# The split weights' second half computed by GpSimd in the mixers, and the vector products' weight tiles loaded by the sync engine

## The chip, the cores and the metric

The kernel runs on one core of a Trainium2 chip. The metric is device time in microseconds (us) for one execution. The kernel before took 3869.05 us (median of three runs, 3862.45 to 3869.21). A core has five engines that each run their own instructions in order: TensorE (PE, matrix products), VectorE (DVE), ScalarE (ACT), GpSimd (POOL) and SyncE (SP, here only a sequencer that issues DMAs). They wait for one another by semaphores. A DMA is an instruction of the engine that issues it, so it stands in that engine's row of work until what it waits for has come.

## The reference

Two blocks in a row, on x of 512 tokens by 1024 features and, in the first block, a context of 256 tokens, all in fp32. Cut to what matters here:

```
for l in 0, 1:                                           # first block
    m_lat = split(silu(c)     @ w_mod[l] + b_mod[l], 6)  # 6 x 1024 numbers: matrix times VECTOR
    m_ctx = split(silu(c_ctx) @ w_mod[l] + b_mod[l], 6)
    h  = rmsnorm(x)  * (1 + m_lat[1]) + m_lat[0]
    hc = rmsnorm(cx) * (1 + m_ctx[1]) + m_ctx[0]
    p, pc = h @ w_in[l], hc @ w_in[l]                    # 30 blocks of 128 columns
    mix = concat(neighbourhood_attention(p), gated_linear_scan(p), gated_conv(p))
    x = x + m_lat[2] * (mix @ w_out[l])
    x = x + m_lat[5] * mixture_of_experts(rmsnorm(x) * (1 + m_lat[4]) + m_lat[3])
    # layer 0: the same for the context
# second block: FFN, differential attention, FFN, shared keys and values,
# FFN, forgetting attention, FFN; each with shifts, scales and gates out of
# silu(c) @ ada_w[layer] (9 x 1024 numbers), one more out of silu(c) @ kv_ada_w
```

## The kernel before, in words

Activations lie transposed, 128 features by the tokens. Each weight projection is done to nearly full fp32 accuracy with three fast products: a weight tile `raw` is rounded by ScalarE into `wh` (L244), its rest `wl = raw - wh` is taken by VectorE (L245), the activation is split the same way, and `mm3` (L247 on) adds `wh*hh + wh*hl + wl*hh` for each 128-row slab (L252, L253, L254). One `split` of 8 slabs makes two pairs of `wh` and `wl`, each 128x512.

A mixer (`mixers`, `mix_in`) is the stage of layer l from `h` to `mix`. `mix_in` runs over 15 loads of 1 MB from `w_in` (`raw`, L117, issued by SyncE, two buffers), two column blocks each. So a mixer has 30 splits, that is 60 roundings and 60 subtractions of 128x512. The `wp` pool holds three pairs (`bufs=3`) of four slabs. Between column blocks run the scan (`hgrn`, lines 676 to 850), the neighbourhood attention (L543 to L601) and the convolution, with much work on VectorE.

The matrix-vector products (`gemv`, L155 to L182) are background work. Each step loads a tile `g` of 128x1024 (512 KB, L166, two buffers), and VectorE multiplies it by the broadcast condition `cb` and sums along the row (L174, output `junk`; 512 wide in the first block, two halves and up to two targets, latent and context, a tile). `fill` inserts steps of these jobs at a set rate between column blocks or FFN tiles: products with `w_mod` in the two mixers and just behind them, with `ada_w` from mixer 1 to FFN 1 (1024 wide there), with `kv_ada_w` near the shared keys and values. `paced` orders each of these instructions behind the last `mm3` matmul issued so far; only the first two loads of a job wait for that matmul on the chip.

The order on each engine comes from the framework's scheduler: the program order with priorities. `later` pushes the splits of `mix_in` back (or the column work as a whole), so that attention and scan go first where both are ready. Once set, each engine runs in that order.

Stages in the profiled execution: mixer 0 to about 500 us, mixture of experts 0 to about 980, mixer 1 to about 1400, mixture of experts 1 to about 1780, then FFN 0 (to 2140), differential attention, FFN 1 (2440 to 2790), keys and values, FFN 2, forgetting attention, FFN 3.

Of the kernel before, what the change touches and what calls it, by code (L numbers as in the profile page):

```python
# [9 lines left out]
F32 = mybir.dt.float32  # L10
# [4 lines left out]
OP = mybir.AluOpType  # L15
# [46 lines left out]
class Net:  # L62
# [95 lines left out]
    def gemv(self, wT, tiles, targets):  # L158


        nc = self.nc
        before = None
        for t in list(tiles) + [None]:
            if t is not None:
                g = self.gp.tile([128, D], F32, tag="g", name="g")
                self.paced(nc.gpsimd.dma_start(g, wT[t]), t - tiles[0] < 2)  # L166
            if before is not None:
                for cb, dst, bias in targets:
                    at = dst[:, before[1]:before[1] + 1]
                    w = self.junk.shape[-1]  # L170
                    part = self.sp.tile([128, 2], F32, tag="part", name="part", bufs=4)
                    for j in range(D // w):
                        js = slice(w * j, w * j + w)
                        self.paced(nc.vector.scalar_tensor_tensor(self.junk, before[0][:, js], 1.0, cb[:, js], op0=OP.mult,  # L174
                                                                  op1=OP.mult, accum_out=part[:, j:j + 1] if w < D else at))
                    if w < D:
                        nc.vector.tensor_add(at, part[:, 0:1], part[:, 1:2])
            if t is None:
                for cb, dst, bias in targets:
                    lo, hi = tiles[0], tiles[-1] + 1  # L180
                    nc.vector.tensor_add(dst[:, lo:hi], dst[:, lo:hi], bias[:, lo:hi])
            before = g, t  # L182
            yield
# [45 lines left out]
                                 self.vec("b_mod0", 0, 16).rearrange("p (j k) -> p j k", k=4))  # L229


    def split(self, src, nk):

        hi, lo = [], []
        for k0 in range(0, nk, 4):
            n = min(4, nk - k0)
            wh, wl = (self.wsplit.tile([128, 4, 128], F32R, tag=n, name=n) for n in ("wh", "wl"))
            self.split_act(src[:, k0:k0 + n], wh[:, :n], wl[:, :n])
            hi += [wh[:, k] for k in range(n)]
            lo += [wl[:, k] for k in range(n)]  # L240
        return hi, lo

    def split_act(self, src, hi, lo):
        self.nc.scalar.activation(hi, src, AF.Copy)  # L244
        self.nc.vector.tensor_tensor(lo, src, hi.bitcast(F32), op=OP.subtract)  # L245

    def mm3(self, out, w, h, ks, first=True, last=True):  # L247
        nc = self.nc
# [181 lines left out]
    def mix_in(self, l, h, hc, na, hg, cv, mix, mixc, need):  # L430
        nc = self.nc
        w = self.a[f"w_in{l}"]
        for f2 in range(15):
            raw = self.raw(w[f2]).rearrange("p (e k m) -> p e k m", e=2, k=8)
            for e in range(2):
                n, p = ORDER[2 * f2 + e]
                ctx = need or n in ("nk", "nv", "hf", "hb", "hi")
                with self.later(-LATER - 400 if l + f2 + e == 0 else -1000):
                    ws = self.split(raw[:, e], 8)
                b, bc = self.bank("m"), self.bank("m")[:, :TC] if ctx else None  # L440
                for ks in (range(4), range(4, 8)):
                    for o, v in ((b, h), (bc, hc)):
                        if o is not None:
                            self.mm3(o, ws, v, ks, ks[0] == 0, ks[-1] == 7)
                if n[0] == "n":
                    for key, s in (("l", b), ("c", bc)):
                        if s is not None:
                            t = na[p][n, key] = self.tmp("ev" if key == "l" else "evc", s.shape[-1])
                            nc.scalar.activation(t, s, AF.Copy)
                elif n[0] == "c":  # L450
                    self.conv(l, n, p, b, bc, cv[p], mix, mixc)
                else:
                    if n in ("hf", "hb"):
                        if n == "hf":
                            hg[p]["z"] = self.tmp("hz", 4 * TA).rearrange("p (s t) -> p s t", s=4)
                        t = hg[p]["z"][:, 0 if n == "hf" else 3]
                    else:
                        t = hg[p][n] = self.tmp(n, TA)
                    for s, sl in ((bc, slice(0, TC)), (b, slice(TC, TA))):
                        if s is None:  # L460
                            continue
                        if n == "hg":
                            nc.scalar.activation(t[:, sl], s, AF.Silu)
                        else:
                            nc.scalar.activation(t[:, sl], s, AF.Copy, scale=0.125 if n == "hq" else 1.0)
                self.fill(self.rate)
                yield
# [1239 lines left out]
```

## Time and profile before

| what | value |
|---|---|
| runs | 3869.05, 3869.21, 3862.45 us |
| profiled execution | 3865.91 us, span 3864.0 us, granted clock 0.965 |
| PE busy | 3628.6 us (94%), 21140 matmuls |
| VectorE busy | 2182.7 us (56%), 5476 instructions |
| ScalarE busy | 1444.8 us (37%) |
| GpSimd busy | 156.0 us (4%), 273 instructions |
| all `wl` on VectorE (L245) | 558.8 us, 826 of them |
| all `wh` on ScalarE (L244) | 512.0 us, 826 of them |
| `g` loads on GpSimd (L166) | 240 of 512 KB |

Busy shares are means over stages that differ: VectorE has 56% in the whole span, but far more in the mixers, and less in the FFNs. PE's records overlap, since matmuls are pipelined, so that its busy share tells little of how much room it has; the number of matmuls in a window tells more. "Idle before" is time in which an engine had nothing to run, with what ended it. A DMA instruction counts as busy only for its issue (about half a us on GpSimd, a third on SyncE); the transfer comes after.

### The profile page before, as it was taken

The page shows a single profiled execution, that of the slowest core. Times are in us where ns is not written, and L with a number is a line of the kernel's source. Part 1 is how long each engine was busy: PE and PEld are TensorE (multiplying, and loading weights), DVE is VectorE, ACT ScalarE, POOL GpSimd, SP SyncE. Part 2 cuts the span into 40 slices and gives each one's busy share as a digit, 9 for nine tenths or more (in the row PEclk, how much of TensorE's full clock was granted, in tenths as well). Part 3 has the DMA queues.
Part 4 walks back from the last instruction along what each step waited for, and adds up shares of the span by engine and source line. Part 5 has one row for each costly group of instructions (what it writes and reads, how often), then busy time and mean ns, then how long its engine had stood idle before and what let it go on. Part 6 is the DMA issues. An engine that isn't in the chain of part 4 may idle for free. (4 is left out here: it accounts for less than half of the span.)

```text
span 3864.0 us, 54771 instructions
## 1 busy us (share of the span) xinstructions
PE 3628.6 (94%) x21140; PEld 2640.8 (68%) x21140; DVE 2182.7 (56%) x5476; ACT 1444.8 (37%) x2826; POOL 156.0 (4%) x273
## 2 busy tenths in 40 slices
PE   7999998999899998988999998999989999999998
PEld 4777784333577775436888676788778887677887
DVE  4999874222689864215566665655643334664334
ACT  4566431111466641113233454322343223553222
POOL 0000000000000000000010000001100000000000
PEclk8999998999899998999999998999999999999999
DMA  5222265777433476994555221455522222012222
GB/s 204 73 80 93 93 209 184 297 278 264 155 118 115 157 238 241 359 344 147 196 196 185 89 77 58 154 191 206 186 76 88 98 103 86 34 55 87 95 96 82
DMA packets 154197, 588.03 MB, mean 152 GB/s; under 512 B 18048, under 2 KB 57256, under 8 KB 111952
## 3 DMA queue, kind: packets, MB, share of 16 engines
q1 hardware_dynamic: 113760, 442.43, 32.0%
q0 software_dynamic: 37872, 137.90, 10.4%
q10 hardware_dynamic: 2304, 4.20, 0.3%
q8 instruction: 166, 2.72, 0.3%
q14 instruction: 95, 0.78, 0.1%
HBM read 575.01 MB, written 9.46 MB: 151 GB/s over the span
## 5 line engine op out<-in xcount | busy, mean ns | idle before, releaser
L244 ACT ACTIVATE wh<-raw 128x512 fp32r<-128x512 f32 (+1 forms) x826 | 512.0, 622 | 1231.9 <-PE m L253 859.0
L245 DVE TENSOR_TENSOR wl<-raw,wh 128x512 fp32r<-128x512 f32 (+1 forms) x826 | 558.8, 678 | 711.0 <-ACT wh L244 698.3
L252 PE MATMUL m<-h,wh 128*128 128x512 f32 x1632 | 658.9, 404 | 26.5 <-DVE t L323 8.4
L253 PE MATMUL m<-h,wh 128*128 128x512 f32 x1632 | 657.7, 403 | 6.2 <-DVE h L326 5.4
L254 PE MATMUL m<-h,wl 128*128 128x512 f32 x1632 | 658.9, 404 | 1.1 <-DVE wl L245 1.1
L174 DVE SCALAR_TENSOR_TENSOR junk<-g,cb 128x512 bf16<-128x512 f32 (+1 forms) x440 | 374.6, 851 | 26.3 <-DMA g<-in_modT 18.5
L252 PEld LDWEIGHTS m<-h,wh 128*128 128x128 f32 x1632 | 313.9, 192 | 99.6 <-ACT h L325 19.0
L253 PEld LDWEIGHTS m<-h,wh 128*128 128x128 f32 x1632 | 312.8, 192 | 81.6 <-DVE h L326 16.5
L254 PEld LDWEIGHTS m<-h,wl 128*128 128x128 f32 x1632 | 312.9, 192 | 68.9 <-issue 7.0
L254 PE MATMUL m<-e,wl 128*128 128x512 f32 x832 | 325.5, 391 | 7.9 <-DVE wl L245 7.9
L252 PE MATMUL m<-e,wh 128*128 128x512 f32 x832 | 325.2, 391 | 0.5 <-ACT wh L244 0.5
L253 PE MATMUL m<-e,wh 128*128 128x512 f32 x832 | 324.7, 390 | 0.0
L252 PE MATMUL f<-h,wh 128*128 128x512 f32 x768 | 299.5, 390 | 0.0
L254 PE MATMUL f<-h,wl 128*128 128x512 f32 x768 | 299.1, 389 | 0.0
L253 PE MATMUL f<-h,wh 128*128 128x512 f32 x768 | 299.0, 389 | 0.0
L1111 PE MATMUL m<-raw,xg 128*64 128x512 f32 (+1 forms) x1264 | 255.0, 603 | 11.0 <-DMA raw<-in_exp_gu 11.0
L254 PEld LDWEIGHTS m<-e,wl 128*128 128x128 f32 x832 | 156.9, 189 | 40.8 <-DVE wl L245 8.3
L1111 PEld LDWEIGHTS m<-raw,xg 128*64 128x64 f32 (+1 forms) x1264 | 63.7, 125 | 173.2 <-issue 146.5
L252 PEld LDWEIGHTS m<-e,wh 128*128 128x128 f32 x832 | 157.1, 189 | 33.4 <-ACT wh L244 1.2
L253 PEld LDWEIGHTS m<-e,wh 128*128 128x128 f32 x832 | 156.9, 189 | 32.7
L254 PEld LDWEIGHTS f<-h,wl 128*128 128x128 f32 x768 | 144.4, 188 | 30.3 <-DVE wl L245 0.3
L252 PEld LDWEIGHTS f<-h,wh 128*128 128x128 f32 x768 | 144.4, 188 | 30.0 <-issue 0.2
(456 smaller groups left out, 5149.9 us busy)
## 6 DMA issues: line engine op xcount, KB each, us to landing
raw<-in_exp_gu SPq DMA_DIRECT2D x98, 1024.0 KB, 6.8
raw<-in_ffn_in SPq DMA_DIRECT2D x88, 1024.0 KB, 4.7
g<-in_adaT POOLq DMA_DIRECT2D x144, 512.0 KB, 4.0
raw<-in_exp_dn SPq DMA_DIRECT2D x48, 1024.0 KB, 6.8
g<-in_modT POOLq DMA_DIRECT2D x80, 512.0 KB, 3.7
raw<-in_w_in SPq DMA_DIRECT2D x30, 1024.0 KB, 4.8
raw<-in_ffn_out SPq DMA_DIRECT2D x32, 896.0 KB, 4.5
raw<-in_ffn_out SPq DMA_DIRECT2D x16, 1024.0 KB, 4.7
```

Of the source, the lines that this page charges most:

```text
L174: self.paced(nc.vector.scalar_tensor_tensor(self.junk, before[0][:, js], 1.0, cb[:, js], op0=OP.mult, op1=OP.mult, accum_out=part[:, j:j + ...
L244: self.nc.scalar.activation(hi, src, AF.Copy)
L245: self.nc.vector.tensor_tensor(lo, src, hi.bitcast(F32), op=OP.subtract)
L252: nc.tensor.matmul(out, wh[k], hh[k], start=(first and k == ks[0]), stop=False)
L253: nc.tensor.matmul(out, wh[k], hl[k], start=False, stop=False)
L254: self.last = nc.tensor.matmul(out, wl[k], hh[k], start=False, stop=(last and k == ks[-1]))
L1111: self.nc.tensor.matmul(out[es, c:c + n], xg[:, es], t, start=start, stop=stop)
```

## The change

Three places. `split` gets an argument `rest`, the engine that takes the subtraction; only `mix_in` gives one, GpSimd. So the 120 subtractions of both mixers move from VectorE to GpSimd; those of the FFNs, attentions and output projections stay. The `g` loads of `gemv` are issued by SyncE in place of GpSimd, all 240 of them, in every stage. The broadcast loads of `cb`, six memsets of `kv` and the indirect row loads of the experts stay on GpSimd.

```diff
@@ gemv
-                self.paced(nc.gpsimd.dma_start(g, wT[t]), t - tiles[0] < 2)
+                self.paced(nc.sync.dma_start(g, wT[t]), t - tiles[0] < 2)
@@ split, split_act
-    def split(self, src, nk):
+    def split(self, src, nk, rest=None):
...
-            self.split_act(src[:, k0:k0 + n], wh[:, :n], wl[:, :n])
+            self.split_act(src[:, k0:k0 + n], wh[:, :n], wl[:, :n], rest)
...
-    def split_act(self, src, hi, lo):
+    def split_act(self, src, hi, lo, rest=None):
         self.nc.scalar.activation(hi, src, AF.Copy)
-        self.nc.vector.tensor_tensor(lo, src, hi.bitcast(F32), op=OP.subtract)
+        (rest or self.nc.vector).tensor_tensor(lo, src, hi.bitcast(F32), op=OP.subtract)
@@ mix_in
-                    ws = self.split(raw[:, e], 8)
+                    ws = self.split(raw[:, e], 8, self.nc.gpsimd)
```

On GpSimd, at the start of mixer 0, the row of instructions changes as follows (L733 clears `kv`, L151 loads the broadcast condition):

```order
+L245 TENSOR_TENSOR wl<-raw,wh 128x512 x3
 L733 MEMSET kv 128x1536
+L245 TENSOR_TENSOR wl<-raw,wh 128x512
 L151 DMA cb<-in_c 128x1024
+L245 TENSOR_TENSOR wl<-raw,wh 128x512 x2
 L151 DMA cb<-in_c_ctx 128x1024
-L166 DMA g<-in_modT 128x1024 x6
+L245 TENSOR_TENSOR wl<-raw,wh 128x512 x13
 L733 MEMSET kv 128x1536
-L166 DMA g<-in_modT 128x1024 x11
```

The subtractions take the places that the `g` loads had, between the same memsets and broadcast loads; GpSimd's row has 38 lines in place of 37.

On SyncE, in the first part of mixer 0 (`nb` are the tables of the attention's bias):

```order
-L117 DMA raw<-in_w_in 128x2048 x5
+L117 DMA raw<-in_w_in 128x2048
+L166 DMA g<-in_modT 128x1024
+L117 DMA raw<-in_w_in 128x2048
+L166 DMA g<-in_modT 128x1024 x2
+L117 DMA raw<-in_w_in 128x2048
+L166 DMA g<-in_modT 128x1024 x3
+L117 DMA raw<-in_w_in 128x2048
+L166 DMA g<-in_modT 128x1024 x3
+L117 DMA raw<-in_w_in 128x2048
+L166 DMA g<-in_modT 128x1024 x4
```

Where the weight loads stood in a row, one to four `g` loads now stand between two of them, and a load behind a `g` load that waits is issued after it. In the FFNs two `g` loads stand between two weight loads.

On VectorE, in mixer 0 around the first gates of the scan (L682 to L701):

```order
-L245 TENSOR_TENSOR wl<-raw,wh 128x512
 L682 SCALAR_TENSOR_TENSOR ls<-hz,ls 128x1536
 L174 SCALAR_TENSOR_TENSOR junk,part<-g,cb 128x512
 L683 TENSOR_TENSOR hz<-ls,hz 128x2x768
 L697 SCALAR_TENSOR_TENSOR hz<-ones,ls 128x128 x12
-L245 TENSOR_TENSOR wl<-raw,wh 128x512
+L174 SCALAR_TENSOR_TENSOR junk,part<-g,cb 128x512
 L700 COPY hsmall<-hz 128x12
-L245 TENSOR_TENSOR wl<-raw,wh 128x512
+L177 TENSOR_TENSOR mlat_82<-part 128x1
+L174 SCALAR_TENSOR_TENSOR junk,part<-g,cb 128x512
```

The subtractions go, and the products with `g` move forward into their places; scan and attention keep their order among themselves.

## Rows read from the trace of the kernel before

**Rows 1.** the page, part 1: busy us, share of the span, instructions.

```profile
PE 3628.6 (94%) x21140; PEld 2640.8 (68%) x21140; DVE 2182.7 (56%) x5476; ACT 1444.8 (37%) x2826; POOL 156.0 (4%) x273
```

**Rows 2.** windows, mixers and FFN 1: length, busy PE PEld DVE ACT POOL, clock, DMA, GB/s.

```profile
87.00:498.00 411.00, 393.03 (x4229) 309.47 (x4229) 382.64 (x1221) 227.05 (x508) 22.82 (x40) 0.99 0.27 92
1050.00:1390.00 340.00, 319.66 (x3093) 245.21 (x3091) 304.55 (x941) 213.68 (x431) 29.80 (x53) 0.97 0.42 142
2450.00:2750.00 300.00, 300.00 (x1325) 248.51 (x1324) 177.24 (x282) 92.82 (x153) 29.56 (x56) 1.00 0.55 194
```

**Rows 3.** lines by form, VectorE, mixer 0: busy us, mean ns, idle before.

```profile
L174 DVE SCALAR_TENSOR_TENSOR junk<-g,cb 128x512 bf16<-128x512 f32 x154 | 105.7, 686 | 0.6
L245 DVE TENSOR_TENSOR wl<-raw,wh 128x512 fp32r<-128x512 f32 x53 | 36.4, 687 | 6.0 <-ACT wh L244 5.8
L816 DVE TENSOR_TENSOR hx<-hz 128x256 f32<-128x256 f32 x63 | 26.6, 422 | 1.9 <-PE s L826 1.6
L818 DVE TENSOR_TENSOR hx<-hz 128x256 f32<-128x256 f32 x63 | 26.6, 422 | 0.1
L820 DVE TENSOR_TENSOR hx<-hx,hq 128x256 f32<-128x256 f32 x63 | 26.5, 422 | 1.0 <-ACT hx L819 0.7
...
L697 DVE TENSOR_TENSOR_SCAN hz<-ones,ls 128x128 f32<-128x128 f32 x36 | 12.0, 402 | 0.0
L586 DVE TENSOR_SCALAR ne<-ne,small 128x512 f32<-128x512 f32 x24 | 11.6, 482 | 0.0
...
L836 DVE TENSOR_TENSOR kt<-s,finemask 128x384 f32<-128x384 f32 x18 | 9.2, 552 | 0.1
...
L552 DVE TENSOR_TENSOR bias<-nb,namask 128x256 f32<-128x256 f32 x16 | 6.6, 414 | 0.2 <-DMA raw<-in_w_in 0.2
```

**Rows 4.** lines by form, VectorE, mixer 1.

```profile
L174 DVE SCALAR_TENSOR_TENSOR junk<-g,cb 128x512 bf16<-128x512 f32 x101 | 69.4, 687 | 7.8 <-DMA g<-in_modT 4.8 <-DMA g<-in_adaT 2.4
L245 DVE TENSOR_TENSOR wl<-raw,wh 128x512 fp32r<-128x512 f32 x54 | 36.9, 687 | 3.7 <-ACT wh L244 3.4 <-ACT mix L764 0.4
L818 DVE TENSOR_TENSOR hx<-hz 128x256 f32<-128x256 f32 x42 | 17.7, 421 | 0.0
```

**Rows 5.** lines by form, PE, mixer 0.

```profile
L252 PE MATMUL m<-h,wh 128*128 128x512 f32 x216 | 89.4, 414 | 6.3 <-ACT hg L463 5.6 <-ACT hi L465 0.6
...
L252 PE MATMUL m<-c,wh 128*128 128x256 f32 x208 | 61.3, 295 | 0.9 <-ACT hg L463 0.9
```

**Rows 6.** lines by form, GpSimd, whole span.

```profile
L166 POOL DMA_DIRECT2D g<-in_adaT x144 | 76.2, 529 | 1186.8 <-DVE junk L174 859.1 <-PE f L254 201.3 <-DMA g<-in_adaT 41.7
...
L733 POOL MEMSET kv<- 128x1536 f32 x6 | 8.3, 1384 | 306.5 <-DVE c L326 238.6 <-PE f L219 34.3 <-PE s L756 33.6
```

**Rows 7.** timeline in mixer 1: start us, us, engine, operation.

```profile
1252.35 0.53 POOL L166 DMA_DIRECT2D g<-in_adaT  x1 [6.68 <-DVE mlat L177]
...
1252.53 0.57 DVE L586 TENSOR_SCALAR ne<-ne,small 128x512 f32<-128x512 f32 x1
```

**Rows 8.** timeline at mixer 1's start.

```profile
1029.53 1.29 DVE L245 TENSOR_TENSOR wl<-raw,wh 128x512 fp32r<-128x512 f32 x2
...
1029.64 1.38 POOL L733 MEMSET kv<- 128x1536 f32 x1 [238.63 <-DVE c L326]
```

**Rows 9.** waits on SyncE and GpSimd, mixer 0: us, times, longest.

```profile
SPq L117 <- DVE wl L245: 243.5, 9, 35.4
...
POOL g L166 <- DVE junk L174: 190.1, 19, 30.0
```

**Rows 10.** waits on SyncE, FFN 1.

```profile
SPq L117 <- DVE wl L245: 287.8, 28, 10.5
```

**Rows 11.** the page, part 6, DMA issues: count, KB, us to landing.

```profile
g<-in_adaT POOLq DMA_DIRECT2D x144, 512.0 KB, 4.0
...
g<-in_modT POOLq DMA_DIRECT2D x80, 512.0 KB, 3.7
raw<-in_w_in SPq DMA_DIRECT2D x30, 1024.0 KB, 4.8
```

## The prediction

> **What bounds the kernel now.** I read the page's first part, then a table of windows, then each engine's lines and waits inside the two mixers. Over the whole span VectorE is busy 56% and PE 94% [rows 1], which suggests that work on VectorE is free. The windows say otherwise: in the mixers VectorE is busy 382.6 of 411 us (93%) and 304.6 of 340 us (90%), in FFN 1 only 177.2 of 300 [rows 2]. There the reader is to see a stage with another limit than the span's. PE's 393.0 of 411 us in mixer 0 looks like a limit too, but its rows overlap: in FFN 1, 1325 matmuls, most of them 128x512, take 300 us, or 0.226 us each. In mixer 0 the three products of some 216 slabs of 512 columns and 208 of 256 are 3 x 216 x 0.226 = 146 us and, at half of that for half the columns, 3 x 208 x 0.113 = 71 us [rows 5]. These 217 us of matmul are half of the window; the many small products of scan and attention take more, but PE is spread out, not full. ScalarE has 227 of 411 us. So VectorE sets the mixers' pace, and a us saved or lost there should count for most of its length. Only these two stages can change much: FFN 1 has VectorE idle for 41%, PE never short of work (300.0 of 300.0), and the change leaves its subtractions alone.
>
> **Part 1, the subtractions: what leaves VectorE.** Each mixer has 60 of them, of 0.687 us [rows 3, 4]: 60 x 0.687 = 41.2 us a mixer, 82.4 in all. With them goes what VectorE waited for roundings ahead of them, 5.8 and 3.4 us, 9 in all [rows 3, 4].
>
> **What GpSimd needs.** No row shows it subtracting. The nearest is the memset of 128x1536, 1.384 us for 1536 elements written per partition [rows 6], 0.90 ns an element. A subtraction of 128x512 reads twice 512 and writes 512. One pass of 512 would be 0.46 us; the two reads one after the other 0.92 us; all three streams, 1536 elements, 1.38 us. I take 1.15, between the last two, as I expect reads to be taken in turn and the write partly beside them. On GpSimd itself this is cheap: 60 x 1.15 = 69 us in 411, beside memsets, and the `g` loads (0.53 us each) are gone from it. PE needs a `wl` several matmuls after its `wh`, and `wp` holds three pairs, so that a `wl` late by one or two us is hidden; without that cover it would cost PE about 0.5 us (1.15 less 0.687) a pair, at most 60 us in all.
>
> The Trainium skill (GPSIMD Engine Reference, section 3.1 Elementwise — side-by-side) gives an fp32 tensor_tensor of 2048 elements 4497 ns on GpSimd and 2293 ns on VectorE, 1.96 times. By that ratio on the 0.687 us the subtraction would be an estimated 1.35 us; no run here shows it, and it lies inside my two ends.
>
> **What it costs VectorE.** Whether the two engines hinder each other is the question on which the sign hangs. The trace has two hints. While GpSimd issues a DMA, a one-input operation of 128x512 took 0.57 us [rows 7] where its usual length is 0.482 [rows 3]: some hindrance, 0.09 us. While GpSimd writes a memset, two subtractions with two inputs on VectorE took 1.29 us together [rows 8], as long as ever: none. Neither has GpSimd reading large operands.
>
> The Trainium skill speaks against the change here (SBUF — State Buffer, section Who interferes with whom): a VectorE instruction with two inputs in SBUF contends with a GpSimd instruction that reads SBUF, not with one that only writes, and the later one waits for the whole of the other. Rows 8 agree with its second half (memset, no delay); nothing here shows the first. Without that rule the memset row would let one expect 82 us of free gain.
>
> As a mechanism of this kernel, with its own numbers: a subtraction on GpSimd that becomes ready gets in between two VectorE instructions, and the next one with two SBUF operands waits until it is through. Of VectorE's remaining 341 us in mixer 0 (382.6 - 41.2) the two-operand groups listed are 105.7 + 26.6 + 26.6 + 26.5 + 12.0 + 9.2 + 6.6 = 213 us, 62% [rows 3]; with the smaller groups of these kinds I take 70%. In mixer 1 the products and the three scan lines are 69.4 + 3 x 17.7 = 122 of 263 us, 46% [rows 4]; with the scans, gates and bias adds beside them, which mixer 0's rows show, I take 65%. So a GpSimd subtraction costs VectorE 0.70 x 1.15 = 0.81 us at once, and where a one-operand instruction (about 0.45 us) ran first, the rest of it: 0.30 x 0.70 x (1.15 - 0.45) = 0.15. That is 0.95 us; in mixer 1 0.65 x 1.15 + 0.35 x 0.65 x 0.70 = 0.91 us.
>
> Mixer 0: 60 x 0.95 = 57 lost, 41 saved: +16 us. Mixer 1: 55 lost, 41 saved: +14 us. With 9 us of waits gone: +21 us of VectorE time. Since VectorE is busy 90 to 93% of the windows, and some of what it loses falls into its idle time, I count 0.7 of it (between one half and nine tenths): **+14 us**. With 0.92 us for the subtraction the same working gives 0.74 and 0.71 us a piece, 44 + 43 - 82 - 9 = -4, or -3 us on the end. With 1.38 us: 1.16 and 1.10 a piece, 70 + 66 - 82 - 9 = +45, or +31 us.
>
> **Part 2, the loads of `g`.** GpSimd issued 240 of them at 0.53 us, 127 us in all [rows 6], time that it had; SyncE has nothing to do but issue. The order is what counts: a weight load now stands behind one to four `g` loads, and these wait until VectorE has used up a `g` tile. Before, SyncE waited 243.5 us in mixer 0 for VectorE to release `raw`, up to 35 us at a time, and GpSimd 190.1 us for products to release `g`, in waits of up to 30 us [rows 9]. Put in one row, a wait costs only if the `g` wait ends after the `raw` wait would have. Both ends follow VectorE's (now for `raw` GpSimd's) order: the products of a `fill` come between column blocks, and the `raw` is free only when its fourth pair has been subtracted, later than the products ahead of it in nearly all places. In FFN 1 SyncE waits for a release in 28 places, 287.8 us [rows 10], so there are ten us a tile in which two `g` loads find room. A weight load of 1 MB lands 4.8 us after its issue, a `g` in 3.7 to 4.0 [rows 11]; behind one another they take longer, and a `g` still has its whole distance of one step to land in. I take 0, bounds -5 and +25 us: the lower end if a weight load was held by nothing and `g` comes sooner, the upper if some five weight loads come late by their landing time each (5 x 4.8).
>
> **Sum.** Profiled execution 3865.9 us (its span 3864.0) + 14 + 0 = 3880 us. The median of the runs shown, 3869.05, is 3 us above that execution; the range takes that in.
>
> **The rivals.**
> *A, the engines do not hinder each other.* Then the 82 us, and 9 of waits, leave VectorE, and the mixers fall to 341 of 411 and 263 of 340 us of VectorE, 83% and 77%, where waits between engines decide more. I count about half: 91 x 0.5 = 45, so 3866 - 45 = 3821 us (3800 to 3845). For it: memset and subtraction side by side at full speed [rows 8]. Against it: the 0.57 us beside a mere DMA issue [rows 7]. It decides as soon as a GpSimd subtraction costs VectorE under 0.6 us. This is the rival of the other sign.
> *B, more is held up than two-operand work.* If every VectorE instruction waits and a subtraction is 1.38 us or more, each costs 1.38 - 0.69 = 0.69 net; 120 x 0.69 = 83, less 9, times 0.7: +52, 3918 us. The row that speaks for it is the same 0.57 us, since that instruction had one input. It decides from about 1.2 us lost per subtraction.
> *C, the shared row of SyncE.* A weight load of a mixer or an early load of the experts stands behind a `g` load whose products are late; PE then waits for `raw`. Five such cost 24 us, and if part 1 is neutral the time is 3890. For it: the GpSimd waits up to 30 us [rows 9]. Against: order and waits as told.
>
> **How the numbers follow.** Chances: the forecast's case 0.46, A 0.33, B 0.11, C 0.10. The predicted time is the forecast's, 3880. Its own range is 3862 to 3900. The range of 8 in 10 runs from A to most of B: 3812 to 3915; it leaves out A's better third and half of B. About 0.2%, or 8 us, is what a measurement here can tell from no change. Faster than that: A (0.32) and a small part of the forecast's case (0.06), 0.38. Within: a share of the forecast's case (0.13), and of A and C (0.04), 0.17. Slower: the rest of the forecast's case (0.27), B (0.11) and C (0.07), 0.45.
>
> **What would show it.** In the profile after: 120 rows of L245 on GpSimd, with 1.0 to 1.4 us each. On VectorE, the means of two-operand lines go up from 0.686 (products) and 0.422 us (scan) by a third or so in mixers, or gaps appear ahead of them, while those of one operand stay at theirs; VectorE's busy share stays above 90%. If those means stay and the mixers are 20 us or more shorter each, A is right and my step on the hindrance is wrong. If one-operand lines stretch too, B. If PE shows waits on `raw`, or SyncE waits of `raw` that end on a product, C. The FFNs should keep their lengths within a few us.

## The result, and the profile after

| kernel | median us | runs | ratio to before (95% interval) |
|---|---|---|---|
| before | 3869.1 | 3862.5 to 3871.0 | |
| changed | 3922.9 | 3916.5 to 3932.5 | 1.0145 (1.0124 to 1.0166) |

The changed kernel is 54 us slower: the sign of the forecast, but about four times its size (+14), and beyond its range. The profiled execution is the slowest of the four (3932.5 us, span 3930.7), so its differences add up to 67 us. Where they arise is read from one operation at the end of each mixer, the router's weights (L910); its row gives count, shortest, median and longest duration in ns, then first and last start. Before, then after:

```profile
L910 DVE TENSOR_TENSOR wa<-router,ms x3: 284/296/297, 497.8 to 1390.0; 128x128 f32<-128x128 f32 x3
```

```profile
L910 DVE TENSOR_TENSOR wa<-router,ms x3: 281/281/281, 532.6 to 1445.5; 128x128 f32<-128x128 f32 x3
```

Mixer 0 ends 34.8 us later. From there to the end of mixer 1 it is 912.9 us where it was 892.2, 20.7 more. What follows mixer 1 adds 11, of which 7 stand in the second mixture of experts. Nothing is gained in any stage.

The page's first part and the windows of the two mixers, as they now stand (length, busy time of PE, PEld, VectorE, ScalarE, GpSimd with counts, clock, DMA share, GB/s), answer to [rows 1, 2]:

```profile
PE 3664.3 (93%) x21140; PEld 2659.6 (68%) x21140; DVE 2200.2 (56%) x5356; ACT 1443.9 (37%) x2826; POOL 206.8 (5%) x153
```

```profile
87.00:533.00 446.00, 409.29 (x4237) 316.75 (x4236) 395.19 (x1172) 226.82 (x508) 77.28 (x52) 0.96 0.25 86
1085.00:1446.00 361.00, 326.49 (x3066) 250.25 (x3067) 314.52 (x883) 209.68 (x428) 80.02 (x53) 0.95 0.37 123
```

In mixer 0 the window is 35 us longer for the same work. PE was busy for 393.0 and idle for 18.0 us of it; now for 409.3 and 36.7. VectorE has 395.2 us, though the 53 subtractions of this window [rows 3] have gone. With them left out and nothing put in their place (e5 below) mixer 0 has 354.4 us of VectorE, so the rest has grown by 41 us. (The records of neighbouring VectorE instructions overlap, so that the 36.4 us of the subtractions cannot simply be taken off the 382.6.) The mean clock fell from 0.99 to 0.96. Of its two levels, 1.2 and 2.4 GHz, the lower then held for 8% of 446 us, 36 us, where it was 2% of 411, 8 us; by this estimate half of the difference, 14 us, is lost to the clock.

VectorE's and GpSimd's lines in mixer 0, by form (busy us, mean ns, idle before and its cause), beside [rows 3, 6]:

```profile
L174 DVE SCALAR_TENSOR_TENSOR junk<-g,cb 128x512 bf16<-128x512 f32 x154 | 108.7, 706 | 0.7
L816 DVE TENSOR_TENSOR hx<-hz 128x256 f32<-128x256 f32 x63 | 30.0, 476 | 6.3 <-PE s L826 5.9
L820 DVE TENSOR_TENSOR hx<-hx,hq 128x256 f32<-128x256 f32 x63 | 29.2, 466 | 2.8 <-ACT hx L819 2.5
L818 DVE TENSOR_TENSOR hx<-hz 128x256 f32<-128x256 f32 x63 | 28.4, 451 | 0.0
L586 DVE TENSOR_SCALAR ne<-ne,small 128x512 f32<-128x512 f32 x24 | 14.7, 612 | 0.3
...
L840 DVE COPY sc<-dg 32x128 f32<-32x128 f32 x36 | 10.9, 303 | 0.4
...
L580 DVE TENSOR_REDUCE small<-f 128x1 f32<-128x256 f32 x24 | 10.0, 417 | 0.0
L177 DVE TENSOR_TENSOR mlat<-part 128x1 f32<-128x1 f32 x39 | 9.9, 253 | 0.3
...
L800 DVE COPY kv<-s 64x256 f32<-64x256 f32 x18 | 7.6, 422 | 2.4 <-PE s L795 2.1
```

```profile
L245 POOL TENSOR_TENSOR wl<-raw,wh 128x512 fp32r<-128x512 f32 x50 | 74.5, 1491 | 344.7 <-ACT wh L244 317.5 <-PE f L491 13.3 <-PE s L826 9.2
```

A subtraction on GpSimd takes 1.49 us, more than the most that I had allowed (1.38) and than the 1.15 taken. The scan's three lines went from 0.422 us to 0.476 (L816), 0.466 (L820) and 0.451 (L818), by 7 to 13% where I had said a third or so. These are means over a few held ones and many that are as before. Two lines with one operand went up as well: L586 from 0.482 to 0.612 us, and the copy of L840 from 216 to 303 ns; its line before was:

```profile
L840 DVE COPY sc<-dg 32x128 f32<-32x128 f32 x36 | 7.8, 216 | 0.4
```

What reads PSUM alone stayed: L580 at 417, L800 at 422 ns. One place shows what happens (timeline: start us, us, engine, line, operation; in brackets the idle time before it and its cause):

```profile
251.94 1.41 POOL L245 TENSOR_TENSOR wl<-raw,wh 128x512 fp32r<-128x512 f32 x1 [6.86 <-ACT wh L244]
...
252.15 1.47 DVE L820 TENSOR_TENSOR hx<-hx,hq 128x256 f32<-128x256 f32 x1
...
253.77 0.36 PE L826 MATMUL s<-hx 64*32 64x32 f32 x32 [2.03 <-DVE hx L820]
```

The subtraction begins 0.21 us before VectorE's L820, a multiplication with two operands in SBUF. L820 ends 0.27 us after the subtraction and takes 1.47 us, its own 0.42 and 1.05 of waiting. PE, which needs its result for the scan (L826), sits idle for 2.03 us. The same happens to an operation that only copies:

```profile
423.25 1.97 DVE L840 COPY sc<-dg 32x128 f32<-32x128 f32 x4
...
423.40 1.26 POOL L245 TENSOR_TENSOR wl<-raw,wh 128x512 fp32r<-128x512 f32 x1 [4.64 <-ACT wh L244]
...
425.27 0.70 PE L762 MATMUL s<-sc,hvt 128*64 128x128 f32 x8 [1.18 <-DVE sc L840]
```

Four small copies took 1.97 us, and PE waited 1.18 us for them. PE's waits for L820 in mixer 0 (us in total, times, longest), before, and then these and those for L840 after:

```profile
PE s L826 <- DVE hx L820: 2.6, 5, 0.7
```

```profile
PE s L826 <- DVE hx L820: 11.6, 15, 2.0
...
PE s L762 <- DVE sc L840: 3.9, 4, 1.2
```

The stretches of the three scans in mixer 0 became longer. About the same work in each, before and after:

```profile
102.00:162.00 60.00, 57.20 (x954) 45.12 (x953) 56.67 (x169) 34.33 (x72) 2.96 (x4) 0.98 0.15 49
222.00:282.00 60.00, 57.02 (x962) 45.16 (x961) 58.88 (x171) 35.48 (x73) 2.97 (x4) 1.00 0.18 64
358.00:417.00 59.00, 56.16 (x932) 44.15 (x930) 56.13 (x173) 31.10 (x61) 2.64 (x5) 1.00 0.18 58
```

```profile
105.00:177.00 72.00, 64.00 (x986) 49.43 (x985) 66.75 (x187) 35.53 (x76) 13.51 (x9) 0.95 0.21 72
237.00:305.00 68.00, 60.51 (x965) 46.70 (x963) 62.76 (x177) 36.08 (x72) 11.04 (x8) 0.95 0.23 80
383.00:450.00 67.00, 60.90 (x920) 47.50 (x919) 59.43 (x178) 29.41 (x59) 9.96 (x7) 0.87 0.17 57
```

Each takes 8 to 12 us more for about the same matmuls, and the clock is at 0.95, 0.95 and 0.87, where it was 0.98 and 1.00. SyncE's row does what the order said: products now hold it up at L166, and the weight loads' own waits are shorter than in [rows 9].

```profile
SPq L166 <- DVE mctx L177: 134.2, 14, 26.1
SPq L117 <- POOL wl L245: 92.4, 12, 18.1
```

None of PE's longer waits in the mixers names a weight load or a rounding, and PE waited for a `wl` of GpSimd once, for 1.7 us.

### The profile page after: what moved, and what is told of

Its sections match the earlier page's. It is cut to its first block, busy times and chain, and to the rows that moved or that the text cites. A ratio compares the mean times of both kernels' runs of the same rounds, so it can differ in the third digit from the quotient of the medians.

```text
span 3930.7 us, 54792 instructions
## 1 busy us (share of the span) xinstructions
PE 3664.3 (93%) x21140; PEld 2659.6 (68%) x21140; DVE 2200.2 (56%) x5356; ACT 1443.9 (37%) x2826; POOL 206.8 (5%) x153
## 4 chain that ended last, share of the span: by engine, by line
PE 74%; DVE 16%; DMA 5%; ACT 2%; issue 2%; SPq 1%; ACTq 0%; DVEq 0%
PE m L253 13%; PE m L254 13%; PE m L252 13%; PE m L1111 9%; PE f L252 4%; PE f L253 4%; PE f L254 4%; DVE junk L174 2%; PE f L351 2%; DMA c<-in_exp_gu 1%; PE f L1059 1%; DVE t L323 1%; PE f L1018 1%; DMA c<-in_exp_dn 1%; DVE h L326 1%
## 5 line engine op out<-in xcount | busy, mean ns | idle before, releaser
L245 DVE TENSOR_TENSOR wl<-raw,wh 128x512 fp32r<-128x512 f32 x706 | 476.4, 676 | 670.4 <-ACT wh L244 661.9
L174 DVE SCALAR_TENSOR_TENSOR junk<-g,cb 128x512 bf16<-128x512 f32 (+1 forms) x440 | 386.2, 878 | 27.5 <-DMA g<-in_modT 21.5
L245 POOL TENSOR_TENSOR wl<-raw,wh 128x512 fp32r<-128x512 f32 x120 | 177.4, 1481 | 880.0 <-ACT wh L244 824.2
```

Of the source, the lines that this page charges most:

```text
L245: (rest or self.nc.vector).tensor_tensor(lo, src, hi.bitcast(F32), op=OP.subtract)
```

## The experiments

"Before" is the same kernel throughout, run beside each group, with medians of 3867.7 to 3869.1 us.

| run | what it has | median us | ratio to before (95% interval) |
|---|---|---|---|
| e1 | subtractions on GpSimd alone | 3937.4 | 1.0192 (1.0166 to 1.0217) |
| e2 | `g` loads on SyncE alone | 3871.2 | 1.0016 (1.0004 to 1.0028) |
| e3 | both, GpSimd writes and doesn't read | 3870.3 | 1.0007 (0.9997 to 1.0016) |
| e4 | e2, and GpSimd subtracts as well | 3960.6 | 1.0242 (1.0220 to 1.0264) |
| e5 | before, no subtraction in the mixers | 3861.2 | 0.9990 (0.9981 to 1.0000) |
| e6 | before, most of the third product left out | 3853.0 | 0.9963 (0.9949 to 0.9977) |
| e7 | both, second column blocks alone | 3885.8 | 1.0050 (1.0033 to 1.0066) |
| e8 | both, FFNs' subtractions instead of the mixers' | 3875.6 | 1.0013 (1.0004 to 1.0023) |
| e9 | both, first column blocks alone | 3899.8 | 1.0075 (1.0058 to 1.0092) |
| e10 | both, one of the two subtractions of a split | 3905.1 | 1.0086 (1.0066 to 1.0106) |
| e11 | changed, products with `g` cut to a quarter | 3920.8 | 1.0140 (1.0123 to 1.0157) |
| e12 | before, products with `g` cut to a quarter | 3865.9 | 0.9991 (0.9981 to 1.0000) |
| e13 | both, 48 subtractions beside the scans alone | 3905.8 | 1.0090 (1.0069 to 1.0111) |
| e14 | both, the 72 others alone | 3887.7 | 1.0051 (1.0034 to 1.0067) |

Theory 1 was that the subtraction holds VectorE up. Theory 2 was the shared row of SyncE (my rival C). The third was that `wl` comes later.

**e1 and e2, the two halves of the change.** The changed kernel with one edit undone in each:

```diff
# e1
-                self.paced(nc.sync.dma_start(g, wT[t]), t - tiles[0] < 2)
+                self.paced(nc.gpsimd.dma_start(g, wT[t]), t - tiles[0] < 2)
# e2
-                    ws = self.split(raw[:, e], 8, self.nc.gpsimd)
+                    ws = self.split(raw[:, e], 8)
```

> Only the subtractions of the mixers go to GpSimd; the g loads stay in GpSimd's row, between the subtractions. Theory 1 (the subtraction holds up VectorE, by 0.7 us each, on operations with one operand in SBUF too, and the stretched chain costs more than that): the whole loss stays, 3905 to 3930 us, and in the mixers VectorE operations that overlap a subtraction take up to 1.1 us longer. Theory 2 (weight loads stand behind g loads in SyncE's row): most of the loss goes, 3865 to 3885 us. Mixed: a loss of 20 to 35 us, unless g loads that wait in GpSimd's row now hold up the subtractions, which would show as PE waiting for wl on GpSimd.

> Only the g loads move, from GpSimd's row to SyncE's; the subtractions stay on VectorE. Theory 1: no change, 3862 to 3877 us, mixers as long as before. Theory 2: the loss is here, 3900 to 3925 us, with PE waiting for roundings whose raw came late. My forecast's term for this part was 0 us, bounds -5 and +25.

The whole loss is in the subtractions. Alone they cost even more than I had expected at most, 70 us where the changed kernel has 54. PE's waits for `wl` on GpSimd are not among e1's longer ones, so the extra is not shown to come from `g` loads between the subtractions; PE waited 26.3 us for L820 over both mixers, 19.3 in the changed kernel and 4.4 before. The loads alone cost 3 us by the medians and 6 by the ratio, at most 11. Theory 2 and rival C fall.

**e3, writing without reading.**

```diff
-        (rest or self.nc.vector).tensor_tensor(lo, src, hi.bitcast(F32), op=OP.subtract)
+        for _ in range(3):
+            m = rest.memset(lo.bitcast(F32), 0.0)      # and a wait for the rounding of hi
```

> As the changed kernel, but in place of each of the 120 subtractions GpSimd clears the same wl tile three times (three writes of 128x512, about 1.4 us together) once the rounding is done. So wl is zero, the rests of the weights are left out; GpSimd reads nothing. SyncE's row and the load on VectorE are those of the changed kernel, and wl comes about as late. Theory 1: the hindrance goes, VectorE operations keep 0.42 and 0.69 us beside GpSimd's work, mixers 15 to 30 us shorter than before each, 3810 to 3840 us. Theory 2, and a third theory (wl that comes 0.8 us later than on VectorE holds PE up): still 3900 us or more.

Neither range came true: 3870 lies between them. The hindrance went: GpSimd's 360 writes took 0.54 us each, 1.61 a tile (later than the subtraction), and the products and scan kept their lengths (the lines' numbers are 6 higher in this kernel):

```profile
L174 DVE SCALAR_TENSOR_TENSOR junk<-g,cb 128x512 bf16<-128x512 f32 x151 | 103.5, 685 | 0.7
...
L826 DVE TENSOR_TENSOR hx<-hx,hq 128x256 f32<-128x256 f32 x63 | 26.2, 421 | 3.4 <-ACT hx L825 3.0
...
L592 DVE TENSOR_SCALAR ne<-ne,small 128x512 f32<-128x512 f32 x24 | 13.1, 546 | 0.3
...
L846 DVE COPY sc<-dg 32x128 f32<-32x128 f32 x36 | 10.5, 291 | 0.4
```

Two operands: 685 and 421 ns, as in [rows 3]. One operand, L586 (here L592) and L840 (here L846): 546 and 291 ns, so mere writes hold these up too (in e2, where GpSimd has almost nothing to do in the mixers, they have 483 and 216). But the time did not fall below before's, where I had expected 3810 to 3840, although VectorE was relieved. So the lateness of `wl` costs nothing, the reading costs 53 us (3923 less 3870), and **with no reading beside it the relief is worth nothing**. VectorE's order is not the cause either: up to the end of mixer 1, 2656 of 2708 instructions stand in the same order in e3 and in the changed kernel. That the relief is worth nothing overturned the forecast's first step, which e5 and e6 test.

**e4, the suspected cost added to the old work.**

```diff
-        (rest or self.nc.vector).tensor_tensor(lo, src, hi.bitcast(F32), op=OP.subtract)
+        self.nc.vector.tensor_tensor(lo, src, hi.bitcast(F32), op=OP.subtract)
+        if rest is not None:
+            rest.tensor_tensor(self.shadow, src, hi.bitcast(F32), op=OP.subtract)
```

> As with the g loads alone on SyncE, wl on VectorE, but GpSimd subtracts the same tiles as well, into a tile that nobody reads. Theory 1: VectorE keeps its 82 us of subtractions and is held up besides, by 120 x 0.7 = 84 us, of which most counts: 3930 to 3960 us, 60 or more above the kernel with the loads alone. Without hindrance: at most 5 us above that kernel (weight loads then wait for GpSimd too).

89 us above e2, at the upper end. Nobody waits for the shadow's result, and up to the end of mixer 1 VectorE runs the instructions of e2 in the order of e2; it can cost only by holding VectorE and by a later release of `raw` and `wh`. The same 120 subtractions on GpSimd cost 38 us more here than in the changed kernel (3960.6 against 3922.9), where VectorE is rid of its own. So beside the hindrance the relief was worth something; what, no run takes apart. PE's waits for a `wl` of VectorE are 5.5 us here.

**e5 and e6, what paces the mixers.**

```diff
# e5: mix_in
-                    ws = self.split(raw[:, e], 8)
+                    ws = self.round_only(raw[:, e], 8)      # wh twice, no subtraction
# e6: mm3 as called by mix_in
-            self.last = nc.tensor.matmul(out, wl[k], hh[k], start=False, stop=(last and k == ks[-1]))
+            if not thin or k == ks[-1]:
+                self.last = nc.tensor.matmul(out, wl[k], hh[k], start=False, stop=(last and k == ks[-1]))
```

> The kernel before, with the 120 subtractions of the mixers left out: no engine computes them, and the third product reads wh in place of wl (so the rests of these weights are left out). VectorE loses 82 us of work and nothing is added anywhere. If VectorE paces the mixers, as my forecast assumed (half of 91 us realised): about 3822 us, 3800 to 3845. If PE with the chain of its dependent operations paces them, as the write-only kernel at 3870 us suggests: 3858 to 3872 us, and VectorE busy near 83% of the mixer windows in the same length.

> The kernel before, where the mixers do the third product wl*hh for one slab of four only (the rest of it is left out); every rounding and subtraction stays, so VectorE's load is unchanged. PE loses three quarters of a third of its 217 us of split products in mixer 0, 54 us, and some 40 us in mixer 1. If VectorE paces the mixers: 3855 to 3870 us. If PE does: 40 to 90 us less, 3780 to 3830.

Taking all 82 us of subtractions from VectorE is worth 7 us (3868.4 less 3861.2; 4 by the ratio), not 45. This is about the most that a place for them outside VectorE could have given. Its mixers, from the first gates to the router:

```profile
87.00:492.00 405.00, 391.08 (x4212) 304.77 (x4210) 354.39 (x1165) 225.62 (x503) 22.80 (x40) 0.99 0.28 95
1046.00:1376.00 330.00, 314.41 (x3062) 243.68 (x3063) 273.70 (x880) 206.96 (x426) 29.10 (x52) 0.98 0.41 141
```

VectorE has 354.4 of 405 us in place of 382.6 of 411: it goes idle instead of going on. In e6, less work for PE gave 15 us (3853.0 against 3868.4), more than a stage paced by VectorE would, and far less than the 40 expected of one paced by PE (in the profiled execution mixer 1 ends 26 us earlier, at 1363.8 for 1390.0, and 16 of these are lost behind it):

```profile
87.00:484.00 397.00, 354.23 (x3912) 273.07 (x3910) 358.86 (x1147) 224.11 (x505) 19.12 (x33) 0.94 0.26 91
1050.00:1364.00 314.00, 281.13 (x2828) 212.31 (x2826) 282.46 (x863) 204.29 (x420) 21.86 (x38) 0.93 0.34 120
```

There PE has 354 us in place of 393, and the granted clock fell from 0.99 to 0.94 and from 0.97 to 0.93, so that part of the gain may have gone to the slower clock. So neither engine's amount of work sets the mixers' length by itself. What remains, by exclusion, is the chain of small dependent operations that goes from engine to engine, with the clock behind it.

**e7, e9 and e10, fewer subtractions, and which.** Each has 60 on GpSimd in place of 120:

```diff
-                    ws = self.split(raw[:, e], 8, self.nc.gpsimd)
+                    ws = self.split(raw[:, e], 8, self.nc.gpsimd if e else None)        # e7
+                    ws = self.split(raw[:, e], 8, None if e else self.nc.gpsimd)        # e9
-            self.split_act(src[:, k0:k0 + n], wh[:, :n], wl[:, :n], rest)
+            self.split_act(src[:, k0:k0 + n], wh[:, :n], wl[:, :n], rest if k0 else None)   # e10
```

> The changed kernel with only every second column block's subtractions on GpSimd (60 in all in place of 120), the others on VectorE. If the hindrance adds up per subtraction: half of the loss above the kernel with the loads alone on SyncE (3871): 3890 to 3903 us. If it came from a saturated stage (GpSimd's row too long for the last few) most of the loss would go: under 3882.

> The changed kernel with the subtractions of the other column block of each pair (the first of each weight load) on GpSimd, 60 in all; the run with the second ones came to 3886 us, 15 above the kernel with the loads alone, where half of the loss would have been 26. If the loss grows faster than the number of subtractions: again 3880 to 3892 us. If it hangs on where they stand, and the first blocks' are the costly ones: 3900 to 3912 us.

> The changed kernel with only the second of the two 128x512 subtractions of every split on GpSimd, the first on VectorE; 60 in all, and never two behind one another on GpSimd. If two in a row are what hurts (VectorE gets one operation in between them, then is held up again): 3871 to 3884 us. If the number alone decides: 3884 to 3900 us.

They lie 17, 31 and 36 us above their before, against 54 for all. e7 and e10 missed both of their ranges, e9 stands at the edge of one. Two in a row are not what hurts, since e10 has none and costs the most. The two halves, e7 and e9, add up to 48 us, so the cost roughly adds, at 0.3 to 0.6 us a subtraction, and depends on which ones move. What about them decides was the question for e13 and e14.

**e8, the same hindrance where PE doesn't wait.**

```diff
-                    w = self.split(r[:, g], 8)                  # ffn
+                    w = self.split(r[:, g], 8, nc.gpsimd)
-                    ws = self.split(raw[:, e], 8, self.nc.gpsimd)   # mix_in
+                    ws = self.split(raw[:, e], 8)
```

> As the changed kernel, but the subtractions of the mixers are on VectorE again, and the 352 of the FFNs' first weights (ffn_in) are on GpSimd. VectorE is idle for 41% there and PE never waits. If a held-up VectorE costs only where PE waits on it: 3865 to 3885 us though three times as many subtractions run on GpSimd and VectorE operations beside them stretch to up to 1.8 us. If each subtraction costs its 0.45 us of the mixers wherever it runs: 352 x 0.45 = 158 us more, over 4000 us.

352 subtractions cost 7 us against before by the medians, 4 more than e2 (by the ratios no more than e2), so 0.01 us each at most. A window of FFN 0 in e8, then VectorE's products from 1830 to 2130 us, then GpSimd's line over the whole span:

```profile
1800.00:2100.00 300.00, 300.00 (x1326) 248.46 (x1325) 148.82 (x205) 92.31 (x152) 109.46 (x80) 1.00 0.53 194
```

```profile
L174 DVE SCALAR_TENSOR_TENSOR junk<-g,cb 128x1024 bf16<-128x1024 f32 x55 | 82.7, 1504 | 1.7 <-DMA g<-in_kvT 1.2
```

```profile
L245 POOL TENSOR_TENSOR wl<-raw,wh 128x512 fp32r<-128x512 f32 x352 | 467.5, 1328 | 1760.9 <-ACT wh L244 1591.0 <-PE f L1059 169.8
```

The products of 128x1024 took 1504 ns, where before has 1219 in that window, so VectorE was held up here too, these 55 by 15.7 us together. That is less per subtraction than in the mixers. PE went on without a gap, 300.0 of 300 us with 1326 matmuls. So this hold-up cost nothing; it costs where PE is waiting for the operation that is held.

**e11 and e12, the load against the chain.**

```diff
-                        js = slice(w * j, w * j + w)
+                        js = slice(w * j, w * j + (w if w == D else w // 4))
```

> The changed kernel, in which each product with g in the first block takes 128 of its 512 columns (three quarters of these products are left out). Some 290 operations on VectorE fall from 0.69 to about 0.2 us, about 140 us less, most of it inside the mixers; the 120 subtractions stay on GpSimd. If the loss comes from VectorE's load (its lost time has to be worked off): it goes altogether, 3860 to 3875 us. If it comes from held-up operations on which PE waits: most of it stays, 3895 to 3920 us.

> The control of that run: the kernel before with the same products cut to a quarter, subtractions on VectorE. As taking 82 us of subtractions from VectorE gave 7 us, taking 140 us of products should give 5 to 15 us: 3853 to 3864. If VectorE's load paces the mixers after all: 3800 to 3830 us.

With far less to do on VectorE (in e12 the 304 products fell from 208.8 to 87.4 us, 121 less where I had expected 140), the changed kernel stays at 3920.8 (3922.9 with the full products), just above the range for held operations, and the kernel before at 3865.9, just above the first of its two ranges. Mixer 0 up to the router's weights (L910 at 524.2 and 493.4 us), VectorE's busy time being the third number pair:

```profile
87.00:524.00 437.00, 400.45 (x4220) 313.28 (x4220) 335.54 (x1174) 225.17 (x505) 75.48 (x52) 0.97 0.24 85
```

```profile
87.00:493.00 406.00, 387.77 (x4220) 304.17 (x4218) 329.45 (x1224) 224.78 (x505) 22.98 (x41) 1.00 0.27 92
```

VectorE has 335.5 of 437 us against 329.5 of 406. With 101 us of slack on VectorE the mixer still ends 31 us late. The lost time is not worked off in VectorE's idle time: it is not the amount of these products that counts but the moment of the hold.

**e13 and e14, beside the scans and elsewhere.** The column blocks were chosen by where their subtractions had stood in the changed kernel's trace:

```diff
-                    ws = self.split(raw[:, e], 8, self.nc.gpsimd)
+                    scan = 2 * f2 + e in (5, 6, 7, 8, 13, 14, 15, 16, 21, 22, 23, 24)
+                    ws = self.split(raw[:, e], 8, self.nc.gpsimd if scan else None)     # e13
+                    ws = self.split(raw[:, e], 8, None if scan else self.nc.gpsimd)     # e14
```

> The changed kernel with only those subtractions on GpSimd that ran beside the scans in its trace: column blocks 5 to 8, 13 to 16 and 21 to 24 of each mixer, 24 subtractions a mixer, 48 in all; the other 72 on VectorE. If the loss comes from held operations that PE waits for in the scans: 35 to 50 us above before though only 40% are moved, 3903 to 3918 us. If every subtraction counts the same: 40% of 51 us above the 3871 of the loads alone, 3886 to 3896 us.

> The opposite: the 72 subtractions outside those blocks on GpSimd, the 48 beside the scans on VectorE. If the loss comes from the scans: 3868 to 3882 us, though 60% are moved. If every subtraction counts the same: 3896 to 3908 us.

The 48 beside the scans cost 38 us, 0.79 each; the 72 others 20 us, 0.28 each. Together 58, near the 54 of all. So the scans carry most of the loss, though more than nothing is left for the rest (e14 lies 6 us above the range that the scans alone would have given). PE's waits for L820 in both mixers, before, in e13 and in e14:

```profile
PE s L826 <- DVE hx L820: 4.4, 8, 0.7
```

```profile
PE s L826 <- DVE hx L820: 23.7, 24, 4.0
```

```profile
PE s L826 <- DVE hx L820: 4.0, 7, 1.0
```

In e13 PE waits 23.7 us for L820, 19 more than before, and this is its longest sum of waits. In e14 it is 4.0 us, as before. The main place in the chain is shown with that: subtraction on GpSimd, L820 on VectorE, L826 on PE. The other half of e13's 38 us, and the 20 of e14, no single wait of PE accounts for.

## Why the prediction was wrong

**The step that failed: "So VectorE sets the mixers' pace, and a us saved or lost there should count for most of its length."** I read a 93% busy share as a bound. e5 (82 us less, 7 us gained), e3 and e12 show that VectorE's work can go without the mixers getting shorter: much of it is the background products and the subtractions, which run ahead of need and fill its gaps. VectorE's own balance came out near the forecast: its busy time rose by 12.6 us in mixer 0 (382.6 to 395.2), where I had +16, and by 10.0 in mixer 1, where I had +14. But the mixers did not grow by 0.7 of that; they grew by 35 and 21 us, more than twice VectorE's whole increase. So the balance of +16 and +14, less 9 of waits, times 0.7, set off a saving that is worth 7 us or less by itself against a loss that counts. Without the saving, the forecast's own 57 + 55 = 112 us held up give 78 us by its factor 0.7, and 56 by the lower one it named, one half. That the last is near the measured 54 is luck: with VectorE's own subtractions in place the hindrance cost 89 us (e4).

**The hindrance was right in kind and nearly in size.** I took 0.95 us per subtraction in mixer 0; the window shows 41 us for the 50 in it, 0.82 each. Its parts were off, to both sides: the subtraction takes 1.48 us on the mean over all 120 (median 1.32, shortest 1.26), not 1.15, so that at 0.82 us each some of them must meet no operation that they can hold. The saving was sized too large as well: leaving the 53 subtractions out took 28 us off VectorE's busy time in mixer 0 (382.6 to 354.4), 0.53 each and not 0.687, since records overlap. And one group that I counted as having two operands in SBUF, L836, reads one of them from PSUM and kept its length (552 and 548 ns); its 9.2 us of 213 change little. That rows 7 hinted at one-operand work was right: L586 and L840 are held, and rival B had this. B's time (3918) is near the result, but its working, 0.69 us net per subtraction with the relief counted in, is not what the runs show.

The Trainium skill's rule (SBUF — State Buffer, section Who interferes with whom) holds here: two-operand instructions wait for a reading GpSimd, up to 1.05 us in the example, and in e3 they don't wait for a writing one. The same section of the Trainium skill lists copies and tensor_scalar as able to contend in their two-port modes; L586 and L840, held by reads and by writes, agree. What the Trainium skill says there of those modes, "Whoever issues first gets the shared pair for the whole instruction", describes the L820 above as well, which ends just after the subtraction. The memset row did not speak for rival A, then, as I had used it, but only for itself.

**GpSimd's own lateness** cost nothing, as forecast (e3). **SyncE's row**: forecast 0 with bounds -5 and +25, measured +3 to +6. **Rival A** is out: had there been no hindrance, e3 says that the time would have been 3870, not 3821. **The FFNs** kept their lengths: from the start of FFN 0 to the end the profiled execution added 4 us.

**What stays open.** Why e1 costs 14 us more than the changed kernel. Why the shadow of e4 costs 38 us more than the changed kernel, though e3 and e5 find hardly any worth in the relief. What the 72 subtractions outside the scans hold up. And what binds the chain before the change: less load on VectorE gives 2 to 7 us, less on PE 15 with a slower clock, and no run shortens the chain itself. How much of the 35 us in mixer 0 is waiting, and how much the clock that falls after it, was only worked out (some 19 and 14 us), not taken apart by a run. Since e5 bounds the gain of another place for the subtractions at about 7 us, no version that beats the kernel before follows from these runs.

## What to carry to other kernels

A busy share of 93% says that an engine has work, not that the work is late: see what of it is background and runs ahead of need before counting its removal as time, and leave the work out in a run of its own (e5) before finding it another engine. Here GpSimd, taking 0.69 us of fp32 two-operand work off VectorE, held VectorE for 0.82 us, in holds of up to about a us that fall on whatever comes next; that is free where PE has a long row of matmuls ahead (e8) and dear where PE waits for small results in a chain (e13). So choose the stage by what waits for VectorE there, not by how busy VectorE is.

## What the runs showed of the hardware that was not expected

Mere writes of GpSimd (0.54 us for 128x512) lengthen VectorE's one-operand operations on SBUF, 0.482 to 0.546 and 0.216 to 0.291 us on the mean (e3), and leave those with two operands alone (421 and 685 ns). A hold hits short operations as hard as long ones: an addition of one column per partition (L177) has a mean of 253 ns in mixer 0 where its usual is 156. The granted clock was lower where PE waited more, though not in step: it fell from 1.00 to 0.87 over the third scan in the changed kernel, with 6.1 us of PE idle for 2.8, but only from 0.98 to 0.95 over the first, with 8.0 for 2.8, and it was 0.93 in mixer 1 when part of PE's work was taken away (e6).
